# Padding the four places of split weights so that all begin in 128-byte rows of one parity

## The chip, the cores and the metric

The kernel runs on one core of a Trainium2 chip. The metric is the device time of one execution in microseconds; lower is better. Before the change the median of three runs is 1669.0 us (1667.32 to 1672.63).

## What is computed

One layer of a decoder for 512 prompt tokens and 64 sample tokens (8 sequences of 8), 576 tokens together, width 1024. Every part is preceded by an RMS norm and a per-sequence shift and scale. In the reference, cut to the lines that make the work:

```python
def swiglu(h, w_gate, w_up, w_down):
    return (jax.nn.silu(h @ w_gate) * (h @ w_up)) @ w_down

def token_mix(h, ...):
    z = h @ w_in                                   # 1024 -> 10240
    u, v, q, k, rv, rg, ga, gb = jnp.split(z, SPLIT_POINTS, axis=-1)
    o_a = gelu(u) * chunk_spatial_mix(layer_norm(gelu(v)))
    o_r, S_new = retention(rotary(q), rotary(k), rv, S0)
    o_b = head_rms(o_r) * silu(rg)
    merged = sigmoid(ga) * (o_a @ w_a) + sigmoid(gb) * (o_b @ w_b)
    return merged @ w_o, S_new, v

m = silu(c) @ w_ada + b_ada                         # shifts, scales and gates
x = x + 0.5 * g1 * swiglu(h1, w1_gate, w1_up, w1_down)
x = x + g2 * token_mix(h2, ...)
x = x + 0.5 * g3 * swiglu(h3, w2_gate, w2_up, w2_down)
```

All of it is float32. The hidden width of the two SwiGLU parts is 2816.

## The kernel before

**Split operands.** A float32 matrix product is made of three products of the `fp32r` type: every operand is kept as a high part (a cast, on ScalarE) and a low part (the rest, on VectorE), and TensorE adds high*high, high*low and low*high. `split_w` (L178) does it for weights in the plain parts, `put_hi` and `put_lo` (L656, L664) in the streamed parts. Both take their room from `whl`.

**Tokens in two halves.** Tokens lie on the free axis. `T` is 576, `H` is 288, and `HALF` (L41) cuts the tokens in two equal halves. One row of 576 tokens takes 2304 bytes of a partition, that is 18 rows of 128 bytes; one half takes 1152 bytes, 9 such rows. "Row" below means 128 bytes of a partition, counted from the partition's start, and its parity is that of the row number.

**Products.** `prod` (L636, matmul in L644) makes one 128 by 288 product over 512 input channels: for each of four blocks j three matmuls, with the weights' high part against the operand's high part, the high part against the low part, and the low part against the high part. The operand lies in tiles `xa` and `xs1` of shape [128, 2, 4, 288]: the two parts are 4608 bytes apart (36 rows), the blocks j 1152 bytes (9 rows). So from one j to the next the moving operand's first row changes its parity, and the first operand row is odd. A streamed pair of blocks (`Pair`, `Pair2`) takes seven such products where the plain way (`Plain`) takes eight (a Strassen scheme). `proj` (L470, matmul in L478) is the plain product of a half of the tokens over kc blocks; there the half, h = 0 or 1, sets the parity of the moving operand's first row. In `values_of` (L1336, matmuls in L1346 and L1359) and `values` (L1559, matmul in L1576) the roles are turned round: tokens (`xx`, `hs`) are the weights of the array, and the split weights are the moving operand, 256 columns.

**Where the split weights lie.** `whl` (L162) takes a tile of tag `whl` from the pool `wp`, which has four places for it, used in turn. A tile holds the high parts and then the low parts, 4096 bytes each as a rule, and begins 28 elements (112 bytes, `INTO`) into its place. A place is 2048 + 28 = 2076 elements, 8304 bytes; the built program puts the four at 46976, 55296, 63616 and 71936 bytes, 8320 bytes or 65 rows apart. Their rows are 367, 432, 497 and 562: odd, even, odd, even. Smaller tiles, `whs`, have one place of their own in another pool, in an even row; `wd`, the weights of the down projections, have two, one odd and one even.

```python
    def set_in(home, shape, room=INTO, **kw):
        ...
        t = home.tile([P, n + room], F32R, **kw)[:, INTO:INTO + n]
```

**What sets the order.** Around the joints between the parts, lists written by hand (`BEGIN`, `INTO_MIX`, `INTO_FFN2`) set the order; elsewhere it is that of the code, with side work started by `tick`. Weights come by DMA on SP's queue into `wraw` (four places), are split into a place of `whl`, and are used by TensorE; the next split of that place waits for TensorE to have read it. Pools on the left side (`wp` and, above it, `xa`, `xs1`, `sn`, `whs`, `raw`, `slt` and others) are stacked; pools on the right side are stacked from the other end.

Of the kernel before, what the change touches and what calls it, by code (L numbers as in the profile page):

```python
# [15 lines left out]
P = 128  # L16
# [21 lines left out]
INTO = 28  # L38
# [43 lines left out]
def layer_kernel(ctx: ExitStack, tc: tile.TileContext, a):  # L82
# [7 lines left out]
    wp = ctx.enter_context(tc.tile_pool(name="wp", bufs=1))  # L90
# [16 lines left out]
    def nm(s):  # L107
        count[0] += 1
        return f"{s}_{count[0]}"


    now = {"wraw": None, "slu": None}
# [31 lines left out]
    def set_in(home, shape, room=INTO, **kw):  # L144

        n = 1
        for d in shape[1:]:
            n *= d
        t = home.tile([P, n + room], F32R, **kw)[:, INTO:INTO + n]
        if len(shape) == 4:  # L150
            return t.rearrange("p (a b c) -> p a b c", b=shape[2], c=shape[3])
        return t.rearrange("p (a b c d) -> p a b c d", b=shape[2], c=shape[3], d=shape[4])
# [9 lines left out]
    def whl(shape):  # L162
        small = len(shape) == 3 and shape[1] == 1
        tag = "whs" if small else "whl"
        return set_in(now["whs"] if small else wp, [P] + shape, tag=tag, name=nm(tag), bufs=1 if small else 4)

    def load_raw(src, k0, kc, c0, cols):
        raw = raw4([kc, cols])
# [5 lines left out]
    def high_low(shape):  # L174
        t = whl([2] + shape)
        return t[:, 0], t[:, 1]
# [479 lines left out]
    class Weights:  # L656
        def put_hi(self, names, src, neg=False):
            hl = whl([2, len(names), 512])
            if neg:
                ACT.activation(out=hl[:, 0], in_=src, func=AF.Copy, scale=-1.0)  # L660
            else:
                ACT.copy(out=hl[:, 0], in_=src)  # L662
            self.hl[names] = hl, src, neg
# [297 lines left out]
    def home_whl(c, shape):  # L961
        return home_wd(c, shape) if c in (0, 1, 4, 5) else whl(shape[1:])
# [1085 lines left out]
```

## Time and profile before

| | before |
|---|---|
| runs, us | 1667.32, 1669.0, 1672.63 |
| span of the profiled execution, us | 1665.5 |
| TensorE matmul busy (PE) | 1636.4 us, 98% |
| weight loads busy (PEld) | 1574.8 us, 95% |
| VectorE busy | 1154.7 us, 69% |
| ScalarE busy | 783.7 us, 47% |
| GpSimd busy | 287.8 us, 17% |
| matmul instructions | 12548 |

The page has no other time of the profiled execution than its span, from the first to the last instruction; the three runs shown are 1.8 to 7.1 us longer. The rows to read are the groups of matmuls (line, output and inputs, columns, count, busy time, mean duration of one). The duration of one is from its start to its modelled end, and runs on under the next matmul: the rate is read from starts, not from durations.

### The profile page before, as it was taken

How to read it: one execution, taken by the hardware profiler on the slowest of the kernel's cores; microseconds unless marked ns; L12 is line 12 of the kernel's file. 1: busy time of each engine (PE TensorE's matmuls, PEld its weight loads, DVE VectorE, ACT ScalarE, POOL GpSimd, SP SyncE). 2: the span in 40 equal slices, each digit the busy share in tenths (PEclk: the TensorE clock that was granted, in tenths of full speed). 3: DMA queues.
4: the chain of work that ended last, by engine and by line, in shares of the span. 5: the costliest groups of instructions: out<-in, count | busy, mean ns of one | idle time of the engine just before them, and what ended most of it. 6: DMA issues, size and time to landing. Idle time of an engine off the chain costs nothing. (4 is left out here: it accounts for less than half of the span.)

```text
span 1665.5 us, 31366 instructions
## 1 busy us (share of the span) xinstructions
PE 1636.4 (98%) x12548; PEld 1574.8 (95%) x12548; DVE 1154.7 (69%) x1835; ACT 783.7 (47%) x1331; POOL 287.8 (17%) x372
## 2 busy tenths in 40 slices
PE   7999999999999999999999999999999999999997
PEld 4899999999999999999999999998999999999997
DVE  6867857576797777755688554677748868576773
ACT  5634524344564566544445454443236535243453
POOL 0000000000411110013346343454231000000002
PEclk9999999999999999999999999999999999999999
DMA  9553444332547676764457474799540333332321
GB/s 301 146 156 102 140 136 130 115 102 87 181 127 219 206 223 198 219 202 153 146 180 251 162 179 151 210 263 267 164 140 14 86 92 99 92 90 85 97 86 58
DMA packets 300212, 252.09 MB, mean 151 GB/s; under 512 B 13593, under 2 KB 260633, under 8 KB 300066
## 3 DMA queue, kind: packets, MB, share of 16 engines
q1 hardware_dynamic: 284594, 206.76, 41.2%
q0 software_dynamic: 13168, 40.97, 8.9%
q10 hardware_dynamic: 2304, 2.36, 0.4%
q8 instruction: 98, 1.61, 0.4%
q14 instruction: 48, 0.39, 0.1%
HBM read 207.01 MB, written 43.02 MB: 150 GB/s over the span
## 5 line engine op out<-in xcount | busy, mean ns | idle before, releaser
L644 PE MATMUL ps<-xa,whl 128*128 128x288 f32 x3000 | 421.0, 295 | 4.4 <-ACT whl L662 1.4
L644 PEld LDWEIGHTS ps<-xa,whl 128*128 128x128 f32 x3000 | 402.0, 189 | 17.3 <-issue 4.2
L644 PE MATMUL ps<-xs,whl 128*128 128x288 f32 x2040 | 289.4, 295 | 0.8 <-ACT sn L653 0.4
L644 PEld LDWEIGHTS ps<-xs,whl 128*128 128x128 f32 x2040 | 274.7, 189 | 10.9 <-issue 5.0
L672 DVE TENSOR_TENSOR whl<-wraw,whl 128x1024 fp32r<-128x1024 f32 x192 | 235.0, 1226 | 55.6 <-ACT whl L662 46.0
L662 ACT CAST whl<-wraw 128x1024 fp32r<-128x1024 f32 x192 | 200.3, 1048 | 109.5 <-DVE wraw L786 67.1
L478 PE MATMUL ps<-c,wd 128*128 128x288 f32 x1824 | 246.1, 295 | 0.0
L478 PEld LDWEIGHTS ps<-c,wd 128*128 128x128 f32 x1824 | 242.4, 189 | 3.7 <-issue 3.4
L478 PE MATMUL ps<-c,whl 128*128 128x288 f32 x1368 | 190.5, 297 | 1.1 <-ACT c L188 0.6
L478 PEld LDWEIGHTS ps<-c,whl 128*128 128x128 f32 x1368 | 182.8, 189 | 3.1 <-ACT c L188 1.1
L465 POOL TENSOR_TENSOR x<-x,s 128x64 f32<-128x64 f32 x72 | 34.6, 481 | 808.2 <-DVE s L464 781.0
L459 DVE SCALAR_TENSOR_TENSOR x<-ps,gate,x 128x288 f32<-128x288 f32 (+1 forms) x128 | 61.2, 481 | 117.1 <-PE ps L478 117.0
L181 DVE TENSOR_TENSOR whl<-wraw,whl 128x1024 fp32r<-128x1024 f32 x56 | 78.0, 1394 | 70.2 <-ACT whl L180 69.4
L653 ACT COPY sn<-ps 128x288 f32<-128x288 f32 x195 | 77.1, 398 | 104.2 <-PE ps L644 103.8
L945 ACT CAST wd<-wraw 128x640 fp32r<-128x640 f32 (+2 forms) x58 | 45.4, 783 | 105.6 <-PE ps L478 97.9
L1346 PE MATMUL ps<-whl,xx 128*128 128x256 f32 x768 | 91.5, 280 | 0.0
L1346 PEld LDWEIGHTS ps<-whl,xx 128*128 128x128 f32 x768 | 90.8, 188 | 0.0
L644 PE MATMUL ps<-xs,whs 128*128 128x288 f32 x480 | 69.8, 294 | 0.0
L180 ACT CAST whl<-wraw 128x1024 fp32r<-128x1024 f32 x56 | 58.5, 1049 | 22.7 <-PE ps L478 14.3
L644 PEld LDWEIGHTS ps<-xs,whs 128*128 128x128 f32 x480 | 65.6, 189 | 0.0
L662 ACT CAST whs<-wraw 128x512 fp32r<-128x512 f32 x62 | 38.4, 620 | 57.0 <-PE ps L644 46.7
L950 DVE TENSOR_TENSOR wd<-wraw,wd 128x640 fp32r<-128x640 f32 (+2 forms) x58 | 53.9, 929 | 9.8 <-ACT wd L945 9.8
(285 smaller groups left out, 2222.2 us busy)
## 6 DMA issues: line engine op xcount, KB each, us to landing
ada<-in_w_ada_dram SPq DMA_DIRECT2D x56, 512.0 KB
wraw<-in_w_in_dram SPq DMA_DIRECT2D x96, 256.0 KB
wraw<-in_w_gate_dram SPq DMA_DIRECT2D x88, 256.0 KB
wraw<-in_w_up_dram SPq DMA_DIRECT2D x88, 256.0 KB
wraw<-in_w_in_dram SPq DMA_DIRECT2D x32, 512.0 KB
wraw<-in_w_down_dram SPq DMA_DIRECT2D x32, 384.0 KB
wraw<-in_w_down_dram SPq DMA_DIRECT2D x32, 320.0 KB
accd<-c POOLq DMA_DIRECT2D x32, 288.0 KB, 6.0
```

The source lines that it names most:

```text
L180: ACT.copy(out=hi, in_=raw)
L181: now["lo"] = (eng or DVE).tensor_tensor(out=lo, in0=raw, in1=hi.bitcast(F32), op=ALU.subtract)
L459: DVE.scalar_tensor_tensor(out=x[:, o:o + w], in0=ps[:, :w], scalar=g[:, c, 0:1], in1=x[:, o:o + w], op0=ALU.mult, op1=ALU.add)
L465: return lambda: POOL.tensor_tensor(out=x[:, NP:T], in0=x[:, NP:T], in1=u, op=ALU.add)
L478: PE.matmul(ps[:, :H], lhsT=s[:, k, c0:c0 + P], rhs=m[:, HALF[h]], start=k == 0 and z == 0, stop=k == kc - 1 and z == 2,)
L644: PE.matmul(ps[:, :H], lhsT=s[:, j * P:(j + 1) * P], rhs=m[:, j, :], start=fresh and j == 0 and z == 0, stop=j == 3 and z == 2, skip_group ...
L653: ACT.copy(out=t, in_=ps[:, :H])
L662: ACT.copy(out=hl[:, 0], in_=src)
L672: now["lo"] = DVE.tensor_tensor(out=hl[:, 1], in0=src, in1=hl[:, 0].bitcast(F32), op=ALU.subtract)
L945: ACT.copy(out=hl[:, 0], in_=self.raw[c])
L950: DVE.tensor_tensor(out=lo, in0=self.raw[c], in1=hi.bitcast(F32), op=ALU.subtract)
L1346: PE.matmul(ps[:, :DV], lhsT=s, rhs=m, start=i == 0, stop=i == 23)
```

## The change

The room beside the 2048 elements of a `whl` tile becomes 64 elements instead of 28. A place is then 2112 elements, 8448 bytes, 66 rows. In the built program the four places begin at 46976, 55424, 63872 and 72320 bytes, in rows 367, 433, 499 and 565, all odd: the first and the third keep their parity, the second and the fourth change it. The tiles still begin 112 bytes into their place, `whs` and `wd` stay as they are, and the left pools above `wp` move by 512 bytes, 4 rows, which leaves their parities alone. The halves of the tokens stay 288 and 288.

```diff
     def whl(shape):
         small = len(shape) == 3 and shape[1] == 1
         tag = "whs" if small else "whl"
-        return set_in(now["whs"] if small else wp, [P] + shape, tag=tag, name=nm(tag), bufs=1 if small else 4)
+        return set_in(
+            now["whs"] if small else wp, [P] + shape, INTO if small else 64, tag=tag, name=nm(tag), bufs=1 if small else 4
+        )
```

No instruction is added, removed or moved on any of the five engines. Since the left pools move by 512 bytes against the right ones, some tiles overlap with other earlier tiles than before, and a few waits go to a neighbouring instruction. On SP, at the start of the token mix after the streamed products, the loads of the retention state (`S`, L1333; two lines further down in the changed file) stand so before:

```order
L1329 DMA hc_8360<-in_hconst_dram 128x338 [waits DMAHW6_49,DMASW7_49]
L1333 DMA S_1078_8362<-in_state_ret_dram 128x2x256 [waits DMASW6_49,DMASW4_49,DMAHW7_49,DMASW2_49,DMASW0_49]
L1333 DMA S_1079_8364<-in_state_ret_dram 128x2x256 [waits DMAHW0_49,DMASW1_49,DMASW0_49]
L1333 DMA S_1080_8366<-in_state_ret_dram 128x2x256 [waits DMAHW1_49,DMASW2_49,Activation_49]
L1333 DMA S_1081_8368<-in_state_ret_dram 128x2x256 [waits DMAHW2_49]
```

and so in the changed program:

```order
L1331 DMA hc_8360<-in_hconst_dram 128x338 [waits DMAHW6_49,DMASW7_49]
L1335 DMA S_1078_8362<-in_state_ret_dram 128x2x256 [waits DMASW6_49,DMASW4_49,DMAHW7_49,DMASW2_49,DMASW0_49]
L1335 DMA S_1079_8364<-in_state_ret_dram 128x2x256 [waits DMAHW0_49,DMASW1_49]
L1335 DMA S_1080_8366<-in_state_ret_dram 128x2x256 [waits DMASW2_49,DMAHW1_49,DMASW0_49,Activation_49]
L1335 DMA S_1081_8368<-in_state_ret_dram 128x2x256 [waits DMAHW2_49]
```

One wait, for a store by GpSimd's queue (DMASW0), went from the second load to the third. Shortly after, on VectorE, the waits for two other such stores stand before at `rvs` (DMASW0 only) and `scs`:

```order
L1364 TENSOR_TENSOR rvs_8504<-ps_8505,h_8522 128x256 [waits DMASW0_49,PE_49,Activation_49]
L181 TENSOR_TENSOR whl_8773<-wraw_8771,whl_8773 128x1024 [waits DMAHW1_49,Activation_49]
L1378 TENSOR_TENSOR c_8568<-ps_8563,hc_8360 128x512 [waits DMAHW6_49,PE_49]
L1385 TENSOR_TENSOR scs_8572<-ps_8570,hc_8360 64x64 [waits DMASW2_49,PE_49]
L1441 COPY S_8631<-ps_8629 128x256 [waits PE_49]
```

and in the changed program at `rvs` (DMASW1 too) and at `S`:

```order
L1366 TENSOR_TENSOR rvs_8504<-ps_8505,h_8522 128x256 [waits DMASW0_49,DMASW1_49,PE_49,Activation_49]
L183 TENSOR_TENSOR whl_8773<-wraw_8771,whl_8773 128x1024 [waits DMAHW1_49,Activation_49]
L1380 TENSOR_TENSOR c_8568<-ps_8563,hc_8360 128x512 [waits DMAHW6_49,PE_49]
L1387 TENSOR_TENSOR scs_8572<-ps_8570,hc_8360 64x64 [waits PE_49]
L1443 COPY S_8631<-ps_8629 128x256 [waits DMASW2_49,PE_49]
```

The rows between `scs` and `S` are left out; they are the same in both. The remaining waits that moved are of the same sort: at the loads of the gates for the merge (L1787), at two MEMSETs on GpSimd (L1291, L1300) and at three later VectorE instructions (L1515, L1830, L459).

## The prediction

> **What bounds the kernel.** I read the head of the page first: span, busy time of each engine, the granted clock in 40 slices.
>
> ```profile
> span 1665.5 us, 31366 instructions
> PE 1636.4 (98%) x12548; PEld 1574.8 (95%) x12548; DVE 1154.7 (69%) x1835; ACT 783.7 (47%) x1331; POOL 287.8 (17%) x372
> PEclk9999999999999999999999999999999999999999
> ```
>
> TensorE is busy for 1636.4 of 1665.5 us, at a granted clock of 0.9 or more in every slice; the weight loads beside it are busy for nearly as long. Next, the longest waits of TensorE:
>
> ```profile
> PE ps L312 <- ACT ada L306: 4.7, 3, 2.0
> PE ps L295 <- ACT ada L292: 4.3, 1, 4.3
> PE ps L1913 <- DVE all L426: 1.8, 1, 1.8
> PE ps L644 <- ACT whl L662: 1.4, 1, 1.4
> PE ps L644 <- DVE whl L672: 1.3, 2, 0.8
> ```
>
> All waits for split weights together are 2.7 us. So the time is the number of matmuls by the spacing of their starts, and nothing that only makes a place ready sooner can be worth more than those 2.7 us. What the change can move is the spacing. The groups of matmuls, each shape apart, say how many there are:
>
> ```profile
> L644 PE MATMUL ps<-xa,whl 128*128 128x288 f32 x3000 | 421.0, 295 | 4.4 <-ACT whl L662 1.4 <-DVE whl L672 1.3 <-ACT xa L557 0.9
> L644 PE MATMUL ps<-xs,whl 128*128 128x288 f32 x2040 | 289.4, 295 | 0.8 <-ACT sn L653 0.4
> L478 PE MATMUL ps<-c,whl 128*128 128x288 f32 x1368 | 190.5, 297 | 1.1 <-ACT c L188 0.6 <-DVE c L189 0.5
> L1346 PE MATMUL ps<-whl,xx 128*128 128x256 f32 x768 | 91.5, 280 | 0.0
> L644 PE MATMUL ps<-xs,whs 128*128 128x288 f32 x480 | 69.8, 294 | 0.0
> L478 PE MATMUL ps<-xx,whl 128*128 128x288 f32 x384 | 54.3, 298 | 0.0
> L1576 PE MATMUL ps<-whl,xx 128*128 128x256 f32 x384 | 47.9, 282 | 0.0
> L644 PE MATMUL ps<-xa,whs 128*128 128x288 f32 x264 | 38.8, 295 | 0.0
> L478 PE MATMUL ps<-xa,whl 128*128 128x288 f32 x96 | 12.9, 295 | 0.0
> L1359 PE MATMUL ps<-whl,hs 128*128 128x256 f32 x128 | 16.4, 281 | 0.0
> L1576 PE MATMUL ps<-whl,hs 128*128 128x256 f32 x64 | 8.4, 284 | 0.0
> ```
>
> The trace holds as many matmuls of each of these lines as the program, in the same order, so the n-th matmul of the trace has the addresses of the n-th of the program. I worked the spacings below out of all starts of these groups, leaving out steps over 160 ns (170 ns within a whole product), where TensorE waited.
>
> **Does an address matter at all?** The weight load for the next matmul runs beside the present one. I sorted the steps of L644 within one weight tile by the distance from the next weights' first row to the present moving operand's first row. At 0, 1, 2 and 3 rows modulo 4 the mean step is 130.0, 132.5, 130.1 and 132.5 ns (1295 to 1363 steps each). So the parity counts, and nothing above it: same parity 130.0, different parity 132.5. By kind of step it is uneven. After high*high (next load: the same weights again) same parity gives 131.9 and different parity 131.2; after high*low (next load: the low part) 127.2 and 133.1; after low*high (next load: the next block's high part) 131.3 and 133.2. The largest gap is 6 ns. Whoever changes parities can win or lose here.
>
> [...]
>
> **What the change does with the parity.** Only the second and the fourth place turn, from even to odd. In a product of L644 the moving operand's first row is odd, even, odd, even for j = 0 to 3, so against an odd place blocks 0 and 2 are of the same parity, against an even place blocks 1 and 3: two and two either way. The timeline of TensorE shows products from both, one after the other:
>
> ```profile
> 683.50 3.31 PE L644 MATMUL ps<-xa,whl 128*128 128x288 f32 x24
> 686.65 3.31 PE L644 MATMUL ps<-xs,whl 128*128 128x288 f32 x24
> 689.80 1.74 PE L644 MATMUL ps<-xa,whl 128*128 128x288 f32 x12
> 691.37 1.74 PE L644 MATMUL ps<-xa,whs 128*128 128x288 f32 x12
> ```
>
> By the program the first 24 matmuls (two products) read place 1, odd; the next 24 read place 2, even; the 12 after them place 4, even; the last 12 `whs`, even. Start to start: 686.65 - 683.50 = 3.15 us, 689.80 - 686.65 = 3.15 us, 691.37 - 689.80 = 1.57 us. Odd and even take the same time. Over all undisturbed products from `whl` the mean is 1576.2 ns from odd places (168 products) and 1576.0 from even ones (172).
>
> **The sum, term by term.** (a) L644: 2520 of the 5040 matmuls with `whl` read the turned places, 210 products; 210 by 0.2 ns = +0.04 us. (b) The joints between products: where the next weights have the other parity than the present ones, a product takes 1577.0 ns (164 of them), where they have the same, 1575.8 (230). In the changed kernel all joints between two `whl` tiles are of the second kind, those with `whs` and others stay mixed. Were all 164 turned, that is 164 by -1.2 ns = -0.20 us; those beside `whs` stay, so I take half, -0.10. (c) L478 with `whl`: 888 of 1848 matmuls turn. There the half of the tokens sets the parity for a whole product, and each weight tile serves both halves. The means are 132.3 ns from odd places and 132.2 from even ones: 888 by 0.1 = +0.09 us. (d) L1346, L1576, L1359: here `whl` is the moving operand, the tokens' rows are fixed (`xx` odd), and there is no second half to pay back. 672 of 1344 matmuls turn. L1346: 117.5 ns from even places and 116.9 from odd, 384 by -0.6 = -0.23 us. L1576: 117.3 and 117.5, 224 by +0.2 = +0.04. L1359: 117.9 and 118.0, nothing. (e) Splits:
>
> ```profile
> L672 DVE TENSOR_TENSOR whl<-wraw,whl 128x1024 fp32r<-128x1024 f32 x192 | 235.0, 1226 | 55.6 <-ACT whl L662 46.0
> L662 ACT CAST whl<-wraw 128x1024 fp32r<-128x1024 f32 x192 | 200.3, 1048 | 109.5 <-DVE wraw L786 67.1
> ```
>
> Sorted by place, L662 takes 1050 ns into even places and 1047 into odd ones (96 each), L672 1226 and 1225. Nothing, and TensorE waits for them 2.7 us in all, which hides a few ns. (f) The waits that moved to a neighbour. The first stand in the stretch from 745 us, the second in the one from 1144 us:
>
> ```profile
> 745.00:760.00 15.00, 14.09 (x120) 13.89 (x120) 8.40 (x10) 6.00 (x10) 6.57 (x12) 1.00 0.93 323
> 1144.00:1165.00 21.00, 19.93 (x146) 19.13 (x145) 16.64 (x30) 6.50 (x10) 5.82 (x5) 1.00 1.05 351
> 743.61 0.54 POOL L1160 DMA_DIRECT2D gad<-c  x1 [2.91 <-ACT c L1155]
> gad<-c POOLq DMA_DIRECT2D x8, 288.0 KB, 2.8
> L1364 DVE TENSOR_TENSOR rvs<-ps,h x8: 410/410/419, 757.9 to 1109.0; 128x256 f32<-128x256 f32 x8
> L1787 SPq EVENT_SEMAPHORE  x21: 17/17/28, 1145.0 to 1163.2; - x21
> ```
>
> The last store of the streamed part is issued at 743.61 and lands 2.8 us later, at about 746.4; the first `rvs`, which now waits for one more such store, starts at 757.9 for other reasons. Behind `rvs` in VectorE's queue stand the next low part of `whl` and then the score products that TensorE's retention work needs, but the store would have to be 11.5 us late to hold them. On SP the wait moves between two loads that follow each other directly, with the `rgd` loads and the next `wraw` behind them; around the gate loads of the merge no wait of SP lasted over 28 ns. I take 0. Bounds: TensorE idles 0.91 and 1.07 us in the two stretches, so no more than 2.0 us can be won; on the other side I put the same 2.0 us, since a delay longer than this idle time has no late releaser in the rows.
>
> Together: 0.04 - 0.10 + 0.09 - 0.23 + 0.04 = -0.2 us, and 0 for (e) and (f). The span goes from 1665.5 to 1665.3 us. The median of the runs lies 3.5 us over this span, so I forecast 1669.0 - 0.2 = **1668.8 us**: no change that can be told.
>
> **Rivals.** *Faster: the turned half gains without paying back.* If the turned matmuls really all went from different to the same parity, 2520 + 888 = 3408 by -2.5 ns would give -8.5 us, 1660.5 us. It is over 0.3% (5.0 us) from about 2000 matmuls on. For it speaks that same parity is the faster class; against it the even two and two in every product and the equal 3.15 us above. It needs a moving operand whose first rows are all of one parity, and with halves of 9 rows there is none.
>
> *Slower: the engines that write the places.* So far, while TensorE reads an odd place, half of the splits write an even one; afterwards every split writes rows laid out as those being read. L672 and L181 have 192 + 56 = 248 splits, each 1.05 + 1.23 = 2.27 us of writing, beside some 17 matmuls: 4290 matmuls, of which half meet this newly. If each lost a class gap, 2145 by 2.5 ns = 5.4 us, 1674.4 us; with the largest gap of 6 ns 12.9 us, 1681.9. It decides from 2.4 ns each. Against it: steps with VectorE and ScalarE both busy throughout are 130.4 ns (same parity) and 132.6 (different), with neither busy 131.7 and 132.6. TensorE does not slow down when they write.
>
> *The change doesn't do what it says.* The built program has all four places in odd rows, so this could only be in that something other than the first row's parity counts; all products would then still be as they are: 1669 us.
>
> **How the numbers follow.** Forecast, with the third case beside it: 0.90. Faster rival 0.05, slower rival 0.05. About 0.3%, 5.0 us, is what a measurement of this kernel can tell from no change. Hence faster 0.05, same 0.90, slower 0.05. Of the range: the unknown waits of (f) give 2.0 us to both sides, and a median of three may differ by some 2 us, since the runs spread from 1667.32 to 1672.63: 1665.0 to 1673.0. The two rivals outside hold 0.10 together.
>
> **What would show it right or wrong.** Two products of 24 matmuls should still take 3.15 us from start to start, from whichever place. Steps after high*low should still be at 127 and 133 ns, in equal numbers. L1346's busy time should stay within 0.5 us of 91.5, PE's within 1 us of 1636.4. Wrong would be: product times of 1570 ns or less (faster rival); L644's busy time up by over 3 us with VectorE's L672 longer than 1226 ns (slower rival); or a new wait of TensorE near 746 to 760 or 1145 to 1165 us.

## The result, and the profile after

The changed kernel takes 1664.63 us (median of ten runs, 1662.34 to 1667.11); the kernel before takes 1669.11 us beside it (ten runs, 1667.31 to 1672.63). The ratio is 0.9972, with a 95% interval of 0.9963 to 0.9982. That is 4.5 us faster, small but clear of zero. The forecast was 1668.8 us and a range from 1665.0 to 1673.0: the time lies 0.4 us below the range. The gain is 0.28%: just under the 0.3% (5.0 us) that the prediction took for the least that can be told from no change, and yet ten runs of each kernel tell it.

The head of the page of the changed kernel shows nothing of it at first sight:

```profile
span 1665.3 us, 31369 instructions
PE 1635.2 (98%) x12548; PEld 1573.8 (95%) x12548; DVE 1155.8 (69%) x1835; ACT 783.9 (47%) x1331; POOL 289.4 (17%) x372
```

The span is 0.2 us shorter than before, not 4.5. The profiled execution is the longest of the ten (1667.11 us), and the reason is in its clock. The windows of TensorE around 448.5, 1134.6 and 1301.8 us, first of the kernel before, then of the changed one (length, busy time and matmuls, granted clock, share of DMA, GB/s):

```profile
448.50:451.90 3.40, 3.40 (x26) 1.00 0.24 87
1134.60:1138.00 3.40, 2.37 (x16) 1.00 0.45 73
1301.80:1305.20 3.40, 2.56 (x17) 1.00 0.10 28
```

```profile
448.50:451.90 3.40, 3.40 (x16) 0.50 0.24 87
1134.60:1138.00 3.40, 3.40 (x16) 0.50 0.68 94
1301.80:1305.20 3.40, 3.23 (x13) 0.51 0.58 171
```

In each of the three the granted clock is half for 3.4 us, and matmuls that ran at full clock before now lose time (16 for 26 in the first). The stretches of 100 us that hold them are 1.4, 1.2 and 1.5 us longer than before. So this profile carries about 4 us that the one before does not. The other nine runs of the changed kernel carry less or as much: their mean granted clock is 0.995 to 0.998, here it is 0.995. Stages are to be compared, not spans.

The groups of matmuls show where the gain is. These rows answer to those shown before (two lines further down in the file):

```profile
L646 PE MATMUL ps<-xa,whl 128*128 128x288 f32 x3000 | 423.6, 296 | 4.4 <-ACT whl L664 1.4 <-DVE whl L674 1.3 <-ACT xa L559 0.9
L646 PE MATMUL ps<-xs,whl 128*128 128x288 f32 x2040 | 289.0, 295 | 0.8 <-ACT sn L655 0.5
L480 PE MATMUL ps<-c,whl 128*128 128x288 f32 x1368 | 191.0, 297 | 1.1 <-ACT c L190 0.6 <-DVE c L191 0.5
L1348 PE MATMUL ps<-whl,xx 128*128 128x256 f32 x768 | 88.9, 276 | 0.0
L1578 PE MATMUL ps<-whl,xx 128*128 128x256 f32 x384 | 46.9, 279 | 0.0
L1361 PE MATMUL ps<-whl,hs 128*128 128x256 f32 x128 | 15.8, 275 | 0.0
L1578 PE MATMUL ps<-whl,hs 128*128 128x256 f32 x64 | 8.2, 280 | 0.0
```

L1346 (now L1348) went from 91.5 to 88.9 us, L1576 over `xx` from 47.9 to 46.9, L1359 from 16.4 to 15.8, L1576 over `hs` from 8.4 to 8.2: -4.4 us of busy time in the stage where the split weights are the moving operand. It is plain in the timeline too. One head's 96 matmuls over `xx` and 16 over `hs`, before and after (start, duration, engine, line, operands, count):

```profile
895.51 11.41 PE L1346 MATMUL ps<-whl,xx 128*128 128x256 f32 x96
906.75 2.05 PE L1359 MATMUL ps<-whl,hs 128*128 128x256 f32 x16
```

```profile
894.57 11.09 PE L1348 MATMUL ps<-whl,xx 128*128 128x256 f32 x96
905.50 1.98 PE L1361 MATMUL ps<-whl,hs 128*128 128x256 f32 x16
```

From the start of the first to the start of the `hs` group it was 11.24 us and is 10.93. In other heads all 112 gain; the single steps, worked out of the starts, show how (ns from start to start, the head after the second one, and the one after it):

```
before, head 2:  117 114 118 121 116 118 117 116 115 117 121 116 121 118 120 118 ...
after,  head 2:  113 113 114 113 113 114 113 113 114 113 113 114 113 113 114 113 ...
after,  head 3:  120 117 119 114 120 120 115 118 121 119 113 114 113 113 114 113 ...
```

Before, the spacing goes up and down between 112 and 124 ns in all heads and places, mean 117.3 over `xx`, and a quarter of the steps are at 115 ns or below. After, 87% are: the stream settles at 113, 113, 114 and stays there, also in the first and the third place, which had not moved. Where other work came in between (head 3) it needs some ten matmuls to settle again. Over the whole stage of 1344 matmuls the time from each start to the next fell from 160.54 to 156.49 us: -4.05 of the 4.5 us. The steps in which TensorE did not wait fell by 4.4 us (117.4 to 114.1 ns, 1326 steps); the rest went into a wait. Twice, near 760 and 860 us, TensorE waits behind matmuls of this stage for GpSimd's rotary product (before, then after: total us, times, longest):

```profile
PE ps L1376 <- POOL c L1324: 1.1, 2, 0.9
PE ps L1378 <- POOL c L1326: 2.1, 2, 1.2
```

TensorE gets there sooner than before, GpSimd's product gains less, and so about 1 us of the gain goes into this wait. The runs below bear it out: the same wait is 1.8 to 2.7 us in those where the stage takes 114 to 115 ns a step throughout, and 1.2 and 1.3 us in the first two that take 117, although these have the changed kernel's places and its moved waits.

The rest of the kernel is nearly as forecast. Two products of 24 matmuls from `whl`, in the timeline of the changed kernel:

```profile
684.01 3.31 PE L646 MATMUL ps<-xa,whl 128*128 128x288 f32 x24
687.16 3.31 PE L646 MATMUL ps<-xs,whl 128*128 128x288 f32 x24
690.30 1.74 PE L646 MATMUL ps<-xa,whl 128*128 128x288 f32 x12
```

3.15 and 3.14 us from start to start, as before.

### The profile page after: what moved, and what is told of

It reads as the page before. It is cut to its first block, busy times and chain, and to the rows that moved or that the text cites. A ratio compares the mean times of both kernels' runs of the same rounds, so it can differ in the third digit from the quotient of the medians.

```text
span 1665.3 us, 31369 instructions
## 1 busy us (share of the span) xinstructions
PE 1635.2 (98%) x12548; PEld 1573.8 (95%) x12548; DVE 1155.8 (69%) x1835; ACT 783.9 (47%) x1331; POOL 289.4 (17%) x372
## 4 chain that ended last, share of the span: by engine, by line
PE 86%; DVE 5%; DMA 4%; ACT 2%; issue 2%; POOL 1%; SPq 0%; POOLq 0%; ACTq 0%; DVEq 0%
PE ps L646 41%; PE ps L480 30%; PE ps L1348 5%; PE ps L1578 3%; PE ps L302 2%; DMA wraw<-in_w_down_dram 1%; ACT whl L664 1%; DVE whl L674 1%; PE ps L1478 1%; DMA xa<-in_w_ada_dram 1%; PE ps L1440 1%; PE ps L1361 1%; PE ps L1484 1%; PE ps L1513 0%; DMA ada<-in_w_ada_dram 0%
## 5 line engine op out<-in xcount | busy, mean ns | idle before, releaser
L674 DVE TENSOR_TENSOR whl<-wraw,whl 128x1024 fp32r<-128x1024 f32 x192 | 234.8, 1224 | 54.3 <-ACT whl L664 44.0
L664 ACT CAST whl<-wraw 128x1024 fp32r<-128x1024 f32 x192 | 200.0, 1047 | 107.2 <-DVE wraw L788 65.6
L461 DVE SCALAR_TENSOR_TENSOR x<-ps,gate,x 128x288 f32<-128x288 f32 (+1 forms) x128 | 61.2, 481 | 117.4 <-PE ps L480 117.3
L1348 PE MATMUL ps<-whl,xx 128*128 128x256 f32 x768 | 88.9, 276 | 0.0
L1348 PEld LDWEIGHTS ps<-whl,xx 128*128 128x128 f32 x768 | 88.2, 188 | 0.0
L182 ACT CAST whl<-wraw 128x1024 fp32r<-128x1024 f32 x56 | 58.5, 1048 | 23.7 <-PE ps L480 15.7
```

The costliest lines, as they stand in the source:

```text
L182: ACT.copy(out=hi, in_=raw)
L461: DVE.scalar_tensor_tensor(out=x[:, o:o + w], in0=ps[:, :w], scalar=g[:, c, 0:1], in1=x[:, o:o + w], op0=ALU.mult, op1=ALU.add)
L674: now["lo"] = DVE.tensor_tensor(out=hl[:, 1], in0=src, in1=hl[:, 0].bitcast(F32), op=ALU.subtract)
L1348: PE.matmul(ps[:, :DV], lhsT=s, rhs=m, start=i == 0, stop=i == 23)
```

## The experiments

Theory after the result, 'stage': the gain is that of the stage with `whl` as moving operand, whose spacing settles at a lower value when its tiles no longer alternate in parity. Rival, 'elsewhere': many small gains in the other 6888 matmuls with `whl`. All experiments are edits of the changed kernel; `into` is the number of elements from the start of a place to the tile, 28 as a rule, and `now["values"]` is true while the weights of that stage are loaded. The distance below is the address of the moving operand's first byte less that of the weights in the array, modulo 256 bytes; in the changed kernel it is 112 in the stage, before it was 112 for odd tiles and 240 for even ones.

**Alternate in the stage alone.**

```diff
+        into = INTO + 32 if now.get("values") and now["place"] % 2 else INTO
+        return set_in(wp, [P] + shape, 64, into, ...)
```

> The changed kernel, but in the stage where split weights are the moving operand (L1346, L1359, L1576; 1344 matmuls of 256 columns) every second weight tile begins 128 bytes later, so that tiles alternate between odd and even rows as before; all other tiles stay odd. Theory 'stage': the whole gain (1669.1 to 1664.6 us, ratio 0.9972) comes from this stage, 1344 matmuls by about -3.1 ns = -4.1 us; so L1346's busy time goes back from 88.9 to about 91.5 us and the time to about 1669, ratio 1.000. Rival 'elsewhere': the gain lies in the other 6888 matmuls with whl, 0.6 ns each; then the ratio stays near 0.997.

1669.18 us, ratio to the kernel before 0.9997 (0.9988 to 1.0006). The gain is gone. The group of L1346 and one head in the timeline:

```profile
L1350 PE MATMUL ps<-whl,xx 128*128 128x256 f32 x768 | 91.6, 280 | 0.0
845.88 11.41 PE L1350 MATMUL ps<-whl,xx 128*128 128x256 f32 x96
```

The group is back at 91.6 us, and a head at 11.41.

**Alternate everywhere else.** The condition is turned round: `not now.get("values") and now["place"] % 2`.

> The reverse of the first: the stage's tiles stay odd, and every second whl tile of all other stages begins 128 bytes later, in even rows. Theory 'stage': the gain stays, ratio 0.997, L1346 at 88.9 us, products of L644 1576 ns as before. Rival 'elsewhere': the gain is gone, ratio 1.000.

1665.61 us, ratio 0.9977 (0.9966 to 0.9988), the group of L1346:

```profile
L1350 PE MATMUL ps<-whl,xx 128*128 128x256 f32 x768 | 88.9, 276 | 0.0
843.68 11.04 PE L1350 MATMUL ps<-whl,xx 128*128 128x256 f32 x96
```

The gain stays. The two runs together place it in the stage. Against 0.9972 for the whole change the run times leave nothing measurable for the other stages.

**All tiles of the stage even.** `into = INTO + 32 if now.get("values") else INTO`.

> The changed kernel, but in the same stage all weight tiles begin 128 bytes later, in even rows, so that the moving operand has one parity throughout, but the other one than the array's weights (xx, odd). Theory 'constancy': what counts is that the parity doesn't switch every 12 matmuls; the steps settle at 113 to 114 ns as in the changed kernel, L1346 about 88.9 us busy, ratio 0.997. Rival 'same parity': only odd with odd is fast, and even ones are slow throughout; steps of 117.5 ns or more, L1346 at 91.5 us or more, ratio 1.000 or above.

1668.62 us, ratio 0.9996 (0.9987 to 1.0006).

```profile
L1350 PE MATMUL ps<-whl,xx 128*128 128x256 f32 x768 | 91.5, 279 | 0.0
896.18 11.41 PE L1350 MATMUL ps<-whl,xx 128*128 128x256 f32 x96
```

'Constancy' falls: with one parity throughout, but the other one, the stage is as slow as with alternation. The steps repeat 114 117 122 116 118 116 117 without end, mean 117.2 ns; in the changed kernel, whose tiles lie 128 bytes from these, it is 114.1. With `xx` in odd rows, the odd tiles are the fast ones.

**Odd and even by pairs.** The offset is switched with each load of two tiles, so that a head of 112 matmuls keeps one parity.

> As the run with all tiles of the stage in even rows, but by pairs: the two weight tiles that one accumulation reads (96 to 112 matmuls in a row) both odd, those of the next load both even, and so on in turn. Theory 'memory': a step's spacing hangs on the steps before it; the odd pairs, left alone for a whole load, settle at 113 to 114 ns as in the changed kernel, although odd tiles between even ones took 116.9; the even pairs stay at 117.5; mean 115.5, L1346 about 90.2 us busy, time about 2 us under the kernel before. Rival 'each step by itself': odd tiles stay at 116.9 and even ones at 117.5, wherever they stand, L1346 at 91.5 us.

One run: 1668.93 us beside 1671.87 for the kernel before. Odd heads have a mean step of 114.2 ns and even ones of 117.3 (663 each). In the timeline an even head and the odd one after it:

```profile
845.11 11.41 PE L1350 MATMUL ps<-whl,xx 128*128 128x256 f32 x96
895.34 11.09 PE L1350 MATMUL ps<-whl,xx 128*128 128x256 f32 x96
```

The odd heads begin at 115 to 121 ns and come down to 113 after seven to eleven matmuls. 'Memory' holds: a tile of the same parity at the same distance takes 116.9 ns a step when it is read for 12 matmuls between even ones, and 113.3 (113, 113, 114) when the stream has had time to settle. The kernel before shows the same from the other side. Sorted by their place among the 12 matmuls of one odd tile, the steps over `xx` have means between 116 and 120 ns for the first nine, and then 115.0, 113.7 and 113.2: the stream has just settled when the even tile comes and it begins anew. In even tiles no place has a mean below 115.8.

**Both operands moved.** Is it the distance or the place itself? The tokens' tiles `xx` were moved by 32 bytes, and by 128, with the `whl` tiles of the stage moved as far (`into` 36 and 60); for the room, the pool of slots has 35 places instead of 36. `hs` stayed, as a control.

```diff
-NSLOT = 36
+NSLOT = 35
-    XT = [xx.tile([P, 2, 2, T], ...) ...]
+    XT = [xx.tile([P, 4 * T + 64], ...)[:, 8:8 + 4 * T].rearrange(...) ...]
```

> In the stage that gained, both operands are moved by 32 bytes against the changed kernel: the tokens' tiles xx begin 32 bytes into an odd row, the weight tiles 16 bytes into an even one, so the distance stays 112 bytes. (For the room, the pool of slots has 35 instead of 36.) The tokens of the samples (hs) stay, distance 144. Theory 'distance': the 1152 matmuls over xx stay locked at 114 ns, those over hs go to 117 or more. Rival 'place in the row': the lock needs the weights to begin at a row and the moving operand 16 bytes ahead of one, as the plain products suggest, where distance 112 alone changed nothing; then xx goes to 117 ns or more too, some 4 us.

> The same with 128 bytes: tokens xx begin at an even row, the weight tiles 112 bytes into an even row; distance 112, and the same places in the row as in the changed kernel, but both parities turned. hs stays at an odd row (distance 240, as in the run with even tiles). Both theories, 'distance' and 'place in the row', say that xx stays locked at 114 ns and hs goes to about 117. Rival 'odd rows': the parity of each by itself counts; then xx goes to 117 ns too.

One head of each (groups over `xx` and over `hs`), the one with 32 bytes first:

```profile
845.46 11.09 PE L1354 MATMUL ps<-whl,xx 128*128 128x256 f32 x96
856.39 2.06 PE L1367 MATMUL ps<-whl,hs 128*128 128x256 f32 x16
```

```profile
846.25 11.09 PE L1354 MATMUL ps<-whl,xx 128*128 128x256 f32 x96
857.17 2.04 PE L1367 MATMUL ps<-whl,hs 128*128 128x256 f32 x16
```

Over `xx` the step is 114.2 ns in both, over `hs` 118.7 and 117.4. So in this stage the distance of 112 decides, not the odd rows and not the place in the row. (One run each, 1667.33 and 1669.37 beside 1669.51 for the kernel before; the reading rests on the steps.)

**Tokens cut at 320.** If 8 rows a matmul settle and 9 don't, the plain products could gain by uneven halves; if the spacing goes with the columns alone, a pair takes the 264.4 ns that two matmuls of 288 columns take.

```diff
+CUT = (slice(0, 320), slice(320, T))
-                    ps[:, :H], lhsT=s[:, k, c0:c0 + P], rhs=m[:, HALF[h]],
+                    ps[:, :n], lhsT=s[:, k, c0:c0 + P], rhs=m[:, cut[h]],
```

> The changed kernel with the tokens cut at 320 instead of 288 in those plain products (L478) whose halves nothing else depends on: 1536 matmuls of 320 columns (10 rows of 128 bytes) and 1536 of 256 (8 rows) for 3072 of 288 (9 rows). The work is the same. [...]

1668.01 us, ratio 0.9992 (0.9982 to 1.0002): by the two ratios some 3.3 us slower than the changed kernel. The steps are 119.4 and 146.9 ns (`whl`), 119.5 and 146.7 (`wd`), so a pair takes 266.3 ns for 264.4, 1536 pairs by 1.9 = +2.9 us. An even number of rows is not enough: the matmuls of 256 columns did not settle, and 320 and 256 columns together take more than two of 288. The 64 columns more cost 27.5 and 27.2 ns; a stream of 256 columns settled at 114 ns would by that have beside it 320 columns at some 141, an estimate from these steps, near the 140 that later expectations name.

**The distance of 112 in the plain products, and 96 in both.** On top of the cut at 320, `whl` tiles of plain loads begin 144 bytes into their place and `wd` tiles in the even place 16 (distance 112); in the second run these and the tiles of the stage are at 96. `wd` tiles in the odd place stay at 144 as a control.

```diff
+        t = whl([2] + shape, 28 if now.get("values") else 36)
+        into = 4 if k[now["hl"]] % 2 else INTO          # wd
```

> The kernel with the tokens cut at 320. In the stage that gained, the moving operand's address less the weights' is 112 modulo 256 bytes; in the plain products L478 it was 144 (or 16). Here the weights of L478 are placed so that it is 112 there too: whl tiles of the plain loads begin 144 bytes into their place (768 pairs of 320 and 256 columns), wd tiles in the even place 16 bytes (384 pairs), wd in the odd place as they were (384 pairs, 144, the control). The stage itself is as in the changed kernel. Theory 'distance of 112 bytes': the lock is a matter of this distance in any stage; L478 settles at about 114 ns (256 columns) and 140 (320) for the 1152 pairs instead of 119.4 and 146.8, 1152 * -12 ns = -14 us against the kernel cut at 320 (1668.0), so 1654 us, ratio 0.991. Rival 'the stage alone': the lock also needs something else that only that stage has; L478 stays at 119 and 147 in all places, ratio 0.999.

> As the one before, with distances of 96 bytes instead of 112 in both stages (values' tiles 96 bytes into an odd row over xx; whl of L478 160 bytes, wd in even places 32 bytes into their place). Theory 'distance', with a window of some width: at 96 bytes both stages still lock, 114 ns. Rival 'a narrow window': as at 128 bytes (118.9 ns in the stage, 118.6 in L478 with 256 columns) the lock is lost, about 117 to 119 ns.

The first takes 1668.22 us, ratio 0.9996 (0.9986 to 1.0006): no better than the cut alone. Steps of `whl` in L478 are 118.8 and 147.0 ns, those of the stage 114.0. With 96 bytes (one run, 1675.9 beside 1669.05) the stage itself goes up to 120.0:

```profile
L1353 PE MATMUL ps<-whl,xx 128*128 128x256 f32 x768 | 93.7, 282 | 0.0
```

So the distance is sharp, and it does not carry over to L478. That is not for want of time: over `xx` in L478, 24 matmuls of 256 columns follow each other at distance 112, and most of them end up at 119 and 121 ns in turn.

**Whole rows.** Two more on the cut at 320, with all `whl` tiles 128 and 256 bytes into their place, distances of 128 and 0 in the stage.

> The kernel with the tokens cut at 320, and all whl tiles begin 128 bytes into their place instead of 112, that is at the start of an even row. In the stage where whl is moving, it is shifted by 16 bytes against the changed kernel, and nearly all of its bytes are in rows of the same parity as there. Theory 'rows': what counts is in which rows the bytes lie, moving operand and weights a row apart; the stage stays at 113 to 114 ns. The same holds for L478 with c (odd row, offset 0) over whl (now even row, offset 0), so these 768 pairs go from 119.4 and 146.9 ns to about 114 and 140, 768 * -12 ns = -9 us against the kernel cut at 320. Rival 'the 112 bytes': the offset inside the row makes the lock; the stage goes back to 117 ns and L478 stays at 119 and 147.

> As the one with 128 bytes, with 256 bytes: all whl tiles begin at the start of an odd row. Theory 'rows': moving operand and weights are now in the same rows' parity in the stage (xx odd, offset 0) as in L478 (c odd, offset 0); 117 ns or more in the stage, 119 and 147 ns in L478 with whl. Rival 'the 112 bytes': no lock either, the same numbers; so this run is the counterpart that shows whether an exact start on a row is worse or better than 112 bytes into it.

One run each: 1681.29 and 1682.38 us beside 1671.87. The stage takes 118.9 and 120.0 ns a step, and the products of L644 133.2 instead of 131.3. 'Rows' falls: 16 bytes more lose the fast spacing. And in L644 too more counts than the parity of the rows, since there the same 16 bytes cost 1.9 ns a matmul.

**Many distances in one run.** Tiles of the stage by load at 112, 108, 116 ..., other `whl` tiles in turn at 0, 16, ... 240 bytes.

> The kernel with the tokens cut at 320, with the weight tiles placed at many distances in one run. In the stage that gained, each load of two tiles has its own distance to xx: 112 twice, 108, 116, 104, 120, 100, 124, and 80, 144, 48, 176 bytes. In all other stages whl tiles begin in turn at 0, 16, 32 ... 240 bytes into their place. Theory 'narrow window' (112 locks, 96 and 128 don't): in the stage 114 ns at 112 and its near neighbours, 117 to 120 at 80, 144, 48, 176. For L478 (c and xx over whl, 48 matmuls of 256 and 48 of 320 columns at each distance): if some distance locks there, it shows as 114 and 140 ns at one or two of the sixteen distances; the rival, that these plain products never settle, gives 117 to 120 and 145 to 148 at all sixteen.

One run, 1677.92 us beside 1667.41. Steps in the stage, by distance: 112 bytes 114.0 ns (191 steps); 108, 116, 104, 120, 100 and 124 bytes 119.7, 121.3, 129.6, 120.3, 120.8 and 117.7; 48, 80, 144 and 176 bytes 118.3, 118.3, 118.7 and 119.3. With 0, 96, 128 and 240 from the other runs, 112 is the only one of 15 distances at which the steps come down to 113 to 114. Most of the others settle too, into a cycle of their own: at 104 bytes 122 and 138 ns in turn, at 0 bytes 120 throughout. In L478 with 256 columns fifteen of the sixteen lie at 116.8 to 119.8. At 192 the mean is 115.8: the 24 matmuls over `xx` as moving operand come down to 113 to 114 within two steps, the 24 over `c` stay at 117 to 118. At 0, 80, 96, 112, 128 and 208 bytes no more than 12 matmuls of 256 columns follow each other in L478 of this run, about as many as the stage needed to settle, so there it could miss a slow settling. With 320 columns all sixteen lie at 145.8 to 147.1.

## Why the prediction was wrong

**The step that failed is term (d)**: "672 of 1344 matmuls turn. L1346: 117.5 ns from even places and 116.9 from odd, 384 by -0.6 = -0.23 us." It rightly said that in this stage "there is no second half to pay back", so the place of the gain was found. But it took each matmul's spacing for a matter of its own address, and sized the change by the mean step of odd places as they then stood. Those odd places were read for 12 matmuls at a time between even ones. The runs show that the spacing hangs on the steps before: odd tiles left alone come down from 116.9 to 113.3 ns (pairs), odd ones between even ones only for the last three of their 12 matmuls (kernel before, and alternation in the stage), and with `xx` in odd rows even ones never do. So all 1344 matmuls gained, 672 that turned and 672 that did not, by 3.3 ns a step instead of 0.3 on half of them: -4.05 us with the longer wait, for -0.19. That the sum of -0.2 us had the right sign is luck: it had this stage at a twentieth of its worth.

That the sum of the stage was measured in a state which the change itself would end was to be seen before. The steps of one place scattered from 112 to 124 ns although all its addresses had one distance modulo 256; a rule by class of address leaves no room for that. The row by position in the odd tile (115.0, 113.7 and 113.2 ns at its end) could have been worked out of the trace before, and 113 was the size of what there was to win. Of the prediction's own signs of being right one fails here: L1346's busy time left 91.5 us by 2.6.

**The other steps.** (a) The two and two of the products in L644 held: 3.15 us for 24 matmuls as before; the mean of the undisturbed products from `whl` fell from 1576.1 to 1574.3 ns (338), 420 products by -1.8 = -0.8 us, where +0.04 had been worked out. In the run that alternates everywhere else it is 1575.9 ns, so this small gain comes from the places too; the mean by place, 1576.2 and 1576.0, did not hold it, as in (d). (b) and (c) are too small to be told apart; the plain products stay at 132.1 to 132.2 ns. (e) The splits take 1047 and 1224 ns for 1048 and 1226. (f) The moved waits cost nothing that shows: the first `rvs` starts at 758.3 us for 757.9, and the longest semaphore wait of its own in VectorE's queue is 50 ns, as before. Of TensorE's waits two grew by over 0.5 us: that for GpSimd in L1376, from 1.1 to 2.1 us, by the faster stage, and one for a load of `w_ada` in the first part (L300, now L302), from 0.4 to 1.2 us.

**The rivals.** The faster one, 8.5 us from all turned matmuls, named the wrong matmuls and the wrong place; the even two and two did speak against it, and did hold. Its condition, "a moving operand whose first rows are all of one parity", is met in just the stage that had been put into (d). The slower one, the engines that write the places, shows nowhere. (One of the four means that the prediction gives against it is off: for steps of the same parity with neither engine busy the trace gives 130.2 to 130.4 ns, by how the edges are taken, not 131.7. That is as much as with both busy and speaks against this rival still more plainly.)

**What stays open.** Why 112 bytes, and why the plain products with the same 256 columns do not settle at 112 (nor `c` at 192, where `xx` does), was not found out; nor was why the products of L644 gain 1.8 ns each. No version tried beats the changed kernel.

## What to carry to other kernels

A mean spacing taken from a stream that switches between two placings did not hold here for a stream that keeps to one of them (odd tiles, 116.9 ns against 113.3): look at the single steps in their order. Odd tiles ended on three steps in a row near 113 ns, and that is what a steady stream reached; even tiles had single steps of 114 ns, but a steady stream of them stayed at a mean of 117.2. Where TensorE sets the time, the stage in which nothing averages out (one operand fixed, the other turned) is the one to size with care, however few its matmuls. And compare stages rather than the spans of two profiles when the granted clock differs in a few windows.

## What the runs showed of the hardware that had not been expected

In the stage, with 256 columns, the spacing has a settled state of 113 to 114 ns. It was reached in some seven to fourteen matmuls, lost when other work came in (then 114 to 123 ns a step) or the distance changed (odd tiles between even ones: mean 116.9 ns), and of 15 distances it was there at 112 bytes alone (mean 114.0 ns): 4 bytes to either side cost 5.7 and 7.3 ns a matmul (119.7 and 121.3), 16 bytes 6.0 and 4.9 (120.0 and 118.9); at a distance of 104 bytes it was 15.6 (129.6). And on one core, in the midst of a kernel whose TensorE is busy for 98% of the span, the granted clock fell to a half for 3.4 us three times in one execution (at 448.5, 1134.6 and 1301.8 us), for a loss of 1.2 to 1.5 us each. In the 3.4 us ahead of each of the three TensorE was busy for 1.82, 2.37 and 1.36 us alone, as it waited for operands. What sets it off was not found out: in the profiled execution before, TensorE was busy for 1.78 of the 3.4 us from 445.1 us on, and the clock stayed at full. That execution had one such window at 28.5 us and none of the three (in both the clock is at half again from 1660 us to the end). Of the fourteen profiled executions six have a half clock near 450 us, three near 1136 us and nine between 1300 and 1316 us.
